# RMS statistics by column groups of TensorE, spread over the partitions by two fp32r products per half

## The chip, the cores and the metric

The kernel runs on one NeuronCore of a Trainium2 chip. The metric is the time of one execution on the device in microseconds. Three timed runs of the kernel before gave 932.94, 933.66 and 934.06 us; the median is 933.66 us.

## The reference

One layer of a two-branch trunk over 1024 tokens of width 1024. What matters here are its two RMS norms, one ahead of everything else and one near the end:

```python
def rms_norm(x, g):
    xf = x.astype(jnp.float32)
    y = xf * lax.rsqrt(jnp.mean(xf * xf, axis=-1, keepdims=True) + NORM_EPS)
    return (y * g.astype(jnp.float32)).astype(x.dtype)

h = rms_norm(x, g_pre[i])
proj = h @ w_in[i]
...
x = x + rms_norm(merged @ w_out[i], g_post[i])
x = x + (p[i] @ w_ple[i]) * jax.nn.sigmoid(x @ w_ple_gate[i])
```

Between them stand the S5 and RG-LRU branches, their projections and gates, which the change leaves alone.

## The kernel before

Activations lie transposed: features over the 128 partitions, tokens along the free dimension, so a row tile of 128 features is 128x1024, and most work goes by halves of 512 tokens. Every large product is made of three fp32r products of 512 columns (`three`, L314 to L318): each operand is split into a rounded high part and a low remainder, and high x high, high x low and low x high are summed in PSUM. Weights come as quads of four 128x128 blocks. ScalarE makes a quad's high part (L222); its remainder comes from VectorE (L234, `lows`) or, for some late weights, from a second copy on ScalarE (L225) followed by an accumulating DMA that GpSimd issues (L226). A quad is prepared four quads ahead of its use.

TensorE, VectorE, ScalarE and GpSimd execute in the order in which the program is written; nothing reorders them. Work that is to run beside products is written as generators, of which `tick()` advances each by one step after a group of products. Only the order of SyncE's DMA issues is chosen by a scheduler.

The mean over features of a norm is a sum over partitions. `tok_rstd` (L383) does it in three steps, separated by `yield`:

1. `pst`: for each 128 tokens one product with the squares `ssq` as the stationary operand and one column of ones as the moving one (L388). The sums of 128 tokens then lie down the 128 partitions of one PSUM column: 128x8 for 1024 tokens, 128x4 for 512.
2. The reciprocal root of these few columns on VectorE and ScalarE: scale and EPS (L392), square root (L393, ScalarE), reciprocal (L394), a Newton step (L395 to L398). Then for each 128 tokens a diagonal matrix of the result (L401).
3. `psb`: ones times each diagonal (L406), which puts the value of each token into all 128 partitions of a PSUM bank, 512 tokens a bank.

It is called in three places.

**Before the first norm** (name `pre`, both halves at once). The squares of the 8 row tiles of `x` are summed on VectorE by seven additions (L710). Meanwhile TensorE computes the eight rows of `p @ w_ple` (`ps_ple`, m = 0 to 7, 12 products each) as filler. Step 1 stands behind row 5, step 3 in the middle of row 7. The rows rotate through three PSUM buffers `pw2`, so row 7 needs the buffer of row 4, which ScalarE must have copied out (`evict(4)`, L740), and the first `ps_u` needs that of row 5. The schedule of ScalarE and VectorE in this stretch is a table:

```python
            4: ((Q, 3), (E, 3)),
            5: ((E, 4), (Q, 4)),
            6: ((E, 5), (Q, 5), (Q, 6)),
```

`Q` prepares a weight quad (L222 and L234), `E` is `evict`. After step 3, `h_hi` scales `x` (L724, VectorE) and makes its high part (L725, ScalarE), `h_lo` its remainder (L730), and the `ps_u` products follow.

**Before the second norm**, by halves of tokens (`post1`, then `post0`), in the generator `post_half`: step 1 and 2 in one tick, step 3 one tick later, which is 12 products of TensorE. Half 1 runs beside the last products `oV` of the output projection; from step 3 on, VectorE normalises, adds the residual and splits eight row tiles (L1559, L1560, L1368, `x1hl`), for which the first gate products `ps_pg` wait. Half 0 runs beside the gate products of half 1, whose sigmoids (L1586) and their use (L1587, L1588) share the engines with it. The square root and the sigmoid need different tables on ScalarE, each loaded by an instruction of its own.

The diagonals of the second norm lie in one page, `diags`.

## Time and profile before

| What | Value |
| --- | --- |
| Median of three runs | 933.66 us (932.94 to 934.06) |
| The profiled execution's own time | 932.99 us |
| Its span, from first to last instruction | 931.2 us |
| VectorE busy | 624.4 us (67%) |
| ScalarE busy | 470.3 us (51%) |
| GpSimd busy | 150.5 us (16%) |
| DMA, mean over the span | 144 GB/s |

The time is 1.8 us longer than the span: that is what lies around the first and the last instruction. A row of the timeline gives the start in the span, the busy time, the engine, the line of the kernel, the instruction, what it writes and reads, the shape and the count of merged instructions, and in brackets for how long the engine stood idle before it and what ended that. An fp32 product shows as two passes in the trace, an fp32r product as one. TensorE's instructions overlap, so their durations are longer than the step from one start to the next.

### The profile page before, as it was taken

Reading aid. Unit: us, or ns where it says so; the run is one execution under the profiler, and the core shown is the slowest. Engines: PE = TensorE matmul, PEld = TensorE weight load, DVE = VectorE, ACT = ScalarE, POOL = GpSimd, SP = SyncE. Lnnn points to the kernel's source line nnn. Section 1 sums busy time; section 2 is a strip of 40 time slices with the busy share of each in tenths; the row PEclk is TensorE's granted clock in tenths of the full one; section 3 lists DMA queues with packets and bytes.
Section 4 is the critical chain, followed back from the end, with each engine's and each line's share of the span. In section 5 each row is a group of like instructions: output and inputs, shape, how many; then the busy total and the mean of one; then the engine's idle time right before and its main releaser. Section 6 shows DMA issues by size and latency. Waiting matters only on the chain.

```text
span 931.2 us, 11720 instructions
## 1 busy us (share of the span) xinstructions
PE 923.2 (99%) x4232; PEld 759.2 (82%) x4232; DVE 624.4 (67%) x974; ACT 470.3 (51%) x714; POOL 150.5 (16%) x159
## 2 busy tenths in 40 slices
PE   8999999999999999999999999999999999999998
PEld 7888888888888888888888888888888887887876
DVE  6885566666664446776666667687862798886863
ACT  6643233444443356666666668544524355558531
POOL 1217112212220000000000000022322126422100
PEclk9999999999999999999999999999999999999999
DMA  9745445554523201111111116811479975499951
GB/s 342 288 126 159 123 144 165 175 166 135 175 95 109 74 29 52 51 50 47 52 51 51 52 39 210 299 39 57 140 259 243 251 180 204 121 244 230 305 176 55
DMA packets 70442, 134.21 MB, mean 144 GB/s; under 512 B 18416, under 2 KB 32880, under 8 KB 70384
## 3 DMA queue, kind: packets, MB, share of 16 engines
q1 hardware_dynamic: 64912, 122.98, 41.3%
q0 software_dynamic: 5472, 10.49, 6.4%
q8 instruction: 33, 0.54, 0.2%
q14 instruction: 25, 0.20, 0.1%
HBM read 95.30 MB, written 27.53 MB: 132 GB/s over the span
## 4 chain that ended last, share of the span: by engine, by line
PE 95%; DVE 3%; DMA 1%; issue 1%; SPq 0%; ACT 0%; DVEq 0%
PE ps_L L318 16%; PE ps_L L316 8%; PE ps_rx L318 8%; PE ps_rg L318 8%; PE ps_pg L318 6%; PE ps_rg L316 4%; PE ps_rx L316 4%; PE ps_F L318 3%; PE ps_u L318 3%; PE bZ L318 3%; PE ps_pg L316 3%; PE pg L318 2%; PE bW L318 2%; PE bX L318 2%; PE ps_ea L318 2%; PE ps_eb L318 2%
## 5 line engine op out<-in xcount | busy, mean ns | idle before, releaser
L318 PE MATMUL ps_L<-hB,wq 128*128 128x512 f32 x640 | 197.4, 390 | 0.0
L318 PEld LDWEIGHTS ps_L<-hB,wq 128*128 128x128 f32 x640 | 120.2, 188 | 24.5
L316 PE MATMUL ps_L<-hB,wq 128*128 128x512 f32 x320 | 127.0, 397 | 0.0
L222 ACT ACTIVATE wq<-wraw 128x512 fp32r<-128x512 f32 (+1 forms) x188 | 112.5, 614 | 23.5 <-issue 9.4
L234 DVE TENSOR_TENSOR wq<-wraw,wq 128x512 fp32r<-128x512 f32 (+1 forms) x152 | 104.2, 701 | 6.4 <-ACT wq L222 6.4
L318 PE MATMUL ps_rx<-hB,wq 128*128 128x512 f32 x320 | 98.6, 390 | 0.0
L318 PE MATMUL ps_rg<-hB,wq 128*128 128x512 f32 x320 | 98.6, 390 | 0.0
L318 PE MATMUL ps_pg<-x1hl,wq 128*128 128x512 f32 x240 | 75.2, 394 | 0.5 <-DVE x1hl L1368 0.5
L316 PEld LDWEIGHTS ps_L<-hB,wq 128*128 128x128 f32 x320 | 60.1, 188 | 13.4 <-issue 1.7
L318 PEld LDWEIGHTS ps_rg<-hB,wq 128*128 128x128 f32 x320 | 60.1, 188 | 12.9
L318 PEld LDWEIGHTS ps_rx<-hB,wq 128*128 128x128 f32 x320 | 60.1, 188 | 12.9
L1072 DVE SCALAR_TENSOR_TENSOR c<-ps_rx,cp_t,c 128x1023 f32<-128x1023 f32 (+2 forms) x30 | 38.5, 1282 | 47.6 <-ACT c L1070 46.9
L194 POOL TENSOR_TENSOR wS<-wraw 128x512 f32<-128x512 f32 x8 | 12.1, 1510 | 356.4 <-DMA wraw<-w_blocks 344.9
L316 PE MATMUL ps_rx<-hB,wq 128*128 128x512 f32 x160 | 62.5, 391 | 0.0
L316 PE MATMUL ps_rg<-hB,wq 128*128 128x512 f32 x160 | 62.5, 391 | 0.0
L318 PEld LDWEIGHTS ps_pg<-x1hl,wq 128*128 128x128 f32 x240 | 44.7, 188 | 11.9 <-DVE x1hl L1368 1.9
L1009 ACT ACTIVATE sg<-ps_L 128x1024 f32<-128x1024 f32 x20 | 20.5, 1027 | 59.6 <-issue 52.4
L226 POOL DMA_DIRECT2D wq<-wraw x36 | 31.8, 882 | 100.7 <-ACT wq L225 68.7
L316 PE MATMUL ps_pg<-x1hl,wq 128*128 128x512 f32 x120 | 47.1, 393 | 0.0
L318 PE MATMUL ps_u<-hB,wq 128*128 128x512 f32 x128 | 39.8, 392 | 0.4 <-DVE hB L730 0.4
L318 PE MATMUL ps_F<-ys,wq 128*128 128x512 f32 x128 | 39.4, 389 | 0.0
L1080 ACT ACT_TABLE_LOAD x9 | 11.5, 1283 | 51.2 <-DVE yr L1109 51.2
(355 smaller groups left out, 1929.7 us busy)
## 6 DMA issues: line engine op xcount, KB each, us to landing
wraw<-w_blocks SPq DMA_DIRECT2D x95, 512.0 KB
wq<-wraw POOLq DMA_DIRECT2D x36, 256.0 KB, 5.8
xt<-x_t SPq DMA_DIRECT2D x8, 512.0 KB
ple_d<-ple_sb SPq DMA_DIRECT2D x8, 512.0 KB
wn<-sbt SPq DMA_DIRECT2D x8, 512.0 KB
sgl_d<-sg SPq DMA_DIRECT2D x8, 512.0 KB
wn<-pt_d SPq DMA_DIRECT2D x16, 256.0 KB
sgs_d<-sg SPq DMA_DIRECT2D x8, 512.0 KB
```

The lines of the kernel that those rows point to most:

```text
L194: G.tensor_tensor(s[name], s[a], s[b], op)
L222: nc.scalar.activation(hi, src, AF.Copy)
L226: nc.gpsimd.dma_start(lo.bitcast(F32), src, accum_op=ALU.add)
L234: self.nc.vector.tensor_tensor(lo, src, hi.bitcast(F32), ALU.subtract)
L316: T.matmul(ps, wh, xh, start=start, stop=False, skip_group_check=more)
L318: T.matmul(ps, a, b, start=False, stop=stop and a is (wh if xl_last else wl), skip_group_check=more)
L1009: S.activation(t, ps, AF.Sigmoid)
L1072: V.scalar_tensor_tensor(c[:, d:], ps[:, :NT - d], w_[3 - d], c[:, d:], ALU.mult, ALU.add)
L1080: S.activation(sq, ps, AF.Sigmoid)
```

## The change

The layout of the statistics is turned round. The sums no longer lie down the partitions but along the free dimension, with ones as the stationary operand and the squares as the moving one:

```diff
-        for c in range(nch):
-            for j, ssq in enumerate(ssqs):
-                T.matmul(ps[:, c:c + 1], ssq[:, c * P:(c + 1) * P], ones[:, 0:1], start=j == 0, stop=j == len(ssqs) - 1)
+        for h in range(nh):
+            for j, src in enumerate(srcs):
+                for c in range(4):
+                    T.matmul(ps[32 * c:32 * c + 32, h * P:(h + 1) * P], ones[:, :32],
+                             src[:, h * HT + c * P:h * HT + (c + 1) * P],
+                             start=j == 0, stop=j == len(srcs) - 1, tile_position=(0, 32 * c), skip_group_check=True)
```

Each product fills 32 partitions of PSUM from one of four groups of 32 columns of the array: tokens 0 to 127 of a half go to partitions 0 to 31, the next 128 to partitions 32 to 63, and so on, every sum 32 times over. The result is 128x128 for a half, 128x256 for both. In the first norm the squares of rows 6 and 7 are no longer added on VectorE but enter as further products: `srcs` has three members, so there are 24 products in place of 8. In the second norm it is four in place of four.

The reciprocal root is then taken of the whole 128x128 or 128x256, in PSUM, by the same instructions:

```diff
-        V.tensor_scalar(var, ps[:, :nch], 1.0 / (ND * P), EPS, ALU.mult, ALU.add)
-        S.activation(sd, var, AF.Sqrt)
-        V.reciprocal(r, sd)
-        V.tensor_tensor(t, r, r, ALU.mult)
-        V.tensor_tensor(t, t, var, ALU.mult)
+        n = nh * P
+        var, t, r = ps[:, :n], ps[:, n:2 * n], r[:, :n]
+        V.tensor_scalar(var, var, 1.0 / (ND * P), EPS, ALU.mult, ALU.add)
+        S.activation(t, var, AF.Sqrt)
+        V.reciprocal(r, t)
+        V.tensor_tensor(t, var, r, ALU.mult)
+        V.tensor_tensor(t, t, r, ALU.mult)
         V.tensor_scalar(t, t, -0.5, 1.5, ALU.mult, ALU.add)
         V.tensor_tensor(r, r, t, ALU.mult)
```

In place of the diagonals, the result is split into an fp32r high part (ScalarE) and a remainder (VectorE) in pieces of 32 partitions x 128, each put at the columns of its tokens in a block of zeros; two fp32r products of 512 columns with a matrix of 1/32 (`sel`) then sum over the partitions and so give every partition the value of each token:

```diff
-        for c in range(nch):
-            V.tensor_scalar(diag[:, c, :], ident, r[:, c:c + 1], None, ALU.mult)
-        yield
-        for h in range(n // HT):
+        for h in range(nh):
+            for c in range(4):
+                s_, cs = slice(32 * c, 32 * c + 32), slice(h * HT + c * P, h * HT + (c + 1) * P)
+                rc = r[s_, h * P:(h + 1) * P]
+                S.activation(hi[s_, cs], rc, AF.Copy)
+                V.tensor_tensor(lo[s_, cs], rc, hi[s_, cs].bitcast(F32), ALU.subtract)
+        yield
+        for h in range(nh):
             pb = px.tile([P, HT], F32, tag="px", name=f"psb_{name}_{h}")
-            for c in range(4):
-                T.matmul(pb[:, c * P:(c + 1) * P], ones, diag[:, 4 * h + c, :], start=True, stop=True)
+            T.matmul(pb, sel, hi[:, h * HT:(h + 1) * HT], start=True, stop=False)
+            T.matmul(pb, sel, lo[:, h * HT:(h + 1) * HT], start=False, stop=True)
```

GpSimd makes `sel` and zeroes the blocks: 128x2048 at the start of the program (page 7, so that the parameters `braw` of the same page are allocated and loaded after the first norm), 128x1024 ahead of the second norm.

ScalarE at the first norm, from the eviction of row 3 (`ps_ple3`) on; `wq` are weight quads. Before:

```order
L740 ACTIVATE ple_sb5_116<-ps_ple3_246 128x1024
L393 ACTIVATE rs_pre_180<-rs_pre_180 128x8
L740 ACTIVATE ple_sb13_117<-ps_ple4_266 128x1024
L222 ACTIVATE wq4_323<-wraw4_196 128x512
L740 ACTIVATE ple_sb13_117<-ps_ple5_284 128x1024
L222 ACTIVATE wq5_341<-wraw4_196 128x512
L222 ACTIVATE wq6_344<-wraw5_220 128x512
```

And after the change, the same place on ScalarE:

```order
L753 ACTIVATE ple_sb5_118<-ps_ple3_250 128x1024
L398 ACTIVATE pst_pre_299<-pst_pre_299 128x256
L409 ACTIVATE spread_122<-sdp_111 32x128 x8
L753 ACTIVATE ple_sb13_119<-ps_ple4_268 128x1024
L222 ACTIVATE wq4_349<-wraw4_200 128x512
L753 ACTIVATE ple_sb13_119<-ps_ple5_286 128x1024
L222 ACTIVATE wq5_367<-wraw4_200 128x512
L222 ACTIVATE wq6_370<-wraw5_224 128x512
```

The eight copies of the high part stand ahead of the eviction of row 4, which before followed the square root at once; they read the end of VectorE's arithmetic.

VectorE at the same place, from the remainder of quad 3 to the first scaling of `x` (L724, now L737). Before:

```order
L234 TENSOR_TENSOR wq3_279<-wraw3_165,wq3_279 128x512
L392 TENSOR_SCALAR rs_pre_180<-pst_pre_297 128x8
L394 RECIPROCAL rs_pre_180<-rs_pre_180 128x8
L395 TENSOR_TENSOR rs_pre_180<-rs_pre_180 128x8
L396 TENSOR_TENSOR rs_pre_180<-rs_pre_180 128x8
L397 TENSOR_SCALAR rs_pre_180<-rs_pre_180 128x8
L398 TENSOR_TENSOR rs_pre_180<-rs_pre_180 128x8
L401 TENSOR_SCALAR sdp_109<-ident_88,rs_pre_180 128x128 x8
L234 TENSOR_TENSOR wq4_323<-wraw4_196,wq4_323 128x512
L234 TENSOR_TENSOR wq5_341<-wraw4_196,wq5_341 128x512
L234 TENSOR_TENSOR wq6_344<-wraw5_220,wq6_344 128x512
L724 SCALAR_TENSOR_TENSOR xt0_107<-xt0_107,cp_t_95,psb_pre_0_354 128x512
```

After:

```order
L397 TENSOR_SCALAR pst_pre_299<-pst_pre_299 128x256
L399 RECIPROCAL sdp_111<-pst_pre_299 128x256
L400 TENSOR_TENSOR pst_pre_299<-pst_pre_299,sdp_111 128x256
L401 TENSOR_TENSOR pst_pre_299<-pst_pre_299,sdp_111 128x256
L402 TENSOR_SCALAR pst_pre_299<-pst_pre_299 128x256
L403 TENSOR_TENSOR sdp_111<-sdp_111,pst_pre_299 128x256
L410 TENSOR_TENSOR spread_122<-sdp_111,spread_122 32x128 x8
L234 TENSOR_TENSOR wq4_349<-wraw4_200,wq4_349 128x512
L234 TENSOR_TENSOR wq5_367<-wraw4_200,wq5_367 128x512
L234 TENSOR_TENSOR wq6_370<-wraw5_224,wq6_370 128x512
L737 SCALAR_TENSOR_TENSOR xt0_109<-xt0_109,cp_t_97,psb_pre_0_380 128x512
```

The count is the same and the place too; each step is 128x256 in place of 128x8, and the eight subtractions each follow one of ScalarE's copies. The remainders of quads 4 to 6 still stand between them and the first scaling.

ScalarE at half 0 of the second norm, where `sbp` is the sigmoid of a gate product. Before:

```order
L393 ACT_TABLE_LOAD
L393 ACTIVATE diags<-diags 128x4
L1586 ACT_TABLE_LOAD
L1586 ACTIVATE sbp<-ps_pg_1_6690 128x512
L222 ACTIVATE wq_6748<-wraw_6581 128x512
```

After:

```order
L398 ACT_TABLE_LOAD
L398 ACTIVATE pst_post_6753<-pst_post_6753 128x128
L409 ACTIVATE spreads<-r_post 32x128 x4
L1600 ACT_TABLE_LOAD
L1600 ACTIVATE sbp<-ps_pg_1_6717 128x512
```

The table load for the sigmoid and the sigmoid itself, which before followed the square root, now follow the four copies.

More of the change, by code (lines that the diff above doesn't have):

```diff
@@ L295, in tile_hybrid_trunk @@
     ident = cst([P, P], "ident")
+    sel = cst([P, P], "sel", dt=F32R)
+    r_post = cst([P, P], "r_post")
     make_identity(nc, ident)
@@ L381, in rows, with tok_rstd @@
         return ps
-    def tok_rstd(v, ssqs, n, name, res, diag):
-        nch = n // P
+    def tok_rstd(r, srcs, n, name, res, spread):
+        nh = n // HT
         ps = px.tile([P, HT], F32, tag="px", name=f"pst_{name}")
-        for c in range(nch):
-            for j, ssq in enumerate(ssqs):
-                T.matmul(ps[:, c:c + 1], ssq[:, c * P:(c + 1) * P], ones[:, 0:1], start=j == 0, stop=j == len(ssqs) - 1)
-        yield
-        v = v.rearrange("p (i n) -> p i n", i=4)
-        var, r, t, sd = (v[:, i, :nch] for i in range(4))
-        V.tensor_scalar(var, ps[:, :nch], 1.0 / (ND * P), EPS, ALU.mult, ALU.add)
-        S.activation(sd, var, AF.Sqrt)
-        V.reciprocal(r, sd)
-        V.tensor_tensor(t, r, r, ALU.mult)
-        V.tensor_tensor(t, t, var, ALU.mult)
+        for h in range(nh):
[4 more added lines that the diff above has]
+                             start=j == 0, stop=j == len(srcs) - 1, tile_position=(0, 32 * c), skip_group_check=True)
+        yield
+        n = nh * P
[5 more added lines that the diff above has]
+        V.tensor_tensor(t, t, r, ALU.mult)
@@ L397, in tok_rstd @@
         V.tensor_scalar(t, t, -0.5, 1.5, ALU.mult, ALU.add)
         V.tensor_tensor(r, r, t, ALU.mult)
-        diag = diag.rearrange("p (c t) -> p c t", c=nch)
-        for c in range(nch):
-            V.tensor_scalar(diag[:, c, :], ident, r[:, c:c + 1], None, ALU.mult)
+        hi, lo = spread
+        for h in range(nh):
[4 more added lines that the diff above has]
+                V.tensor_tensor(lo[s_, cs], rc, hi[s_, cs].bitcast(F32), ALU.subtract)
@@ L476, in tile_hybrid_trunk @@
     pt = scratch[:, :NPT]
-    braw = page(7, "braw", F32)
+    spread = page(7, "spread").rearrange("p (i n) -> p i n", i=2)
     ET = mybir.EngineType
@@ L490, in tile_hybrid_trunk @@
     tq = sk.tile([P, 4, 32], F32, name="tq")
+    G.tensor_scalar(sel, ones, 1.0 / 32.0, None, ALU.mult)
+    zeros = spread.rearrange("p i n -> p (i n)")
+    G.memset(zeros.bitcast(F32), 0.0)
+    G.tensor_copy(zeros, zeros.bitcast(F32))
     G.memset(toep, 0.0)
@@ L705, in square @@
         if k:
-            adds.append(sq)
+            (adds if k < 6 else srcs).append(sq)
     def add_squares(left):
@@ L712, in tile_hybrid_trunk @@
     rb = []
-    ssqs = [ssq]
-    stats = tok_rstd(pro.tile([P, 4 * ND], F32, name="rs_pre"), ssqs, NT, "pre", rb, sdp[:, 1])
+    srcs = [ssq]
+    stats = tok_rstd(sdp[:, 1], srcs, NT, "pre", rb, (spread[:, 0], spread[:, 1]))
     hq = {}
@@ L778, in tile_hybrid_trunk @@
     h_hi(1)
+    braw = page(7, "braw", F32)
     nc.sync.dma_start(braw[:, :1024], spar[:, NPT:NPT + 1024])
@@ L1546, in post_half @@
         add_square(h)
-        st = tok_rstd(dg[:, 2, 32 * h:32 * h + 32], [ssq[h]], HT, f"post{h}", out_, dg[:, h, :])
+        st = tok_rstd(r_post, [ssq[h]], HT, f"post{h}", out_, (dg[:, 0, :], dg[:, 1, :]))
         if h == 0:
@@ L1601, in gate_half @@
                 finish(ps, cs)
-    dg = quarter(page(PG[1], "diags", F32))
+    dg = quarter(page(PG[1], "spreads"))
+    G.memset(dg[:, :2, :].bitcast(F32), 0.0)
+    G.tensor_copy(dg[:, :2, :], dg[:, :2, :].bitcast(F32))
     bg.append(post_half(1))
```

## The prediction

> **What bounds the kernel now.** The page's head comes first.

> ```profile
> span 931.2 us, 11720 instructions
> PE 923.2 (99%) x4232; PEld 759.2 (82%) x4232; DVE 624.4 (67%) x974; ACT 470.3 (51%) x714; POOL 150.5 (16%) x159
> ```

> TensorE (PE) is busy for 923.2 of 931.2 us. So what lengthens or shortens TensorE's own row of work counts in full, a new wait of TensorE counts in full, and there are no later waits in which a delay could vanish. What the other engines do counts only where TensorE comes to wait for it. I therefore read the timeline at the three places of the change, and ask at each what TensorE meets next. The first norm:

> ```profile
> 22.43 2.55 DVE L710 TENSOR_TENSOR sdp<-sdp,sqs 128x1024 f32<-128x1024 f32 x2
> 25.04 1.95 PE L388 MATMUL pst_pre<-ones,sdp 128*128 128x1 f32 x16
> 26.84 0.48 PE L316 MATMUL ps_ple<-p_hi,wq 128*128 128x512 f32 x1
> 27.02 0.17 DVE L392 TENSOR_SCALAR rs_pre<-pst_pre 128x8 f32<-128x8 f32 x1 [1.43 <-PE pst_pre L388]
> 27.22 0.21 ACT L393 ACTIVATE rs_pre<-rs_pre 128x8 f32<-128x8 f32 x1 [3.49 <-DVE rs_pre L392]
> 27.34 1.01 ACT L740 ACTIVATE ple_sb<-ps_ple 128x1024 f32<-128x1024 f32 x1
> 28.51 1.67 DVE L401 TENSOR_SCALAR sdp<-ident,rs_pre 128x128 f32<-128x128 f32 x8
> 29.67 1.15 ACT L222 ACTIVATE wq<-wraw 128x512 fp32r<-128x512 f32 x2
> 30.08 1.90 DVE L234 TENSOR_TENSOR wq<-wraw,wq 128x512 fp32r<-128x512 f32 x3
> 31.04 1.95 PE L406 MATMUL psb_pre<-sdp,ones 128*128 128x128 f32 x16
> 32.13 1.64 DVE L724 SCALAR_TENSOR_TENSOR xt<-xt,cp_t,psb_pre 128x512 f32<-128x512 f32 x2 [0.15 <-PE psb_pre L406]
> 39.29 0.74 PE L318 MATMUL ps_u<-hB,wq 128*128 128x512 f32 x2 [0.40 <-DVE hB L730]
> ```

> The whole arithmetic (27.02 to 30.18) lies beside 18 row products, 26.84 to 31.04, 0.233 us each, and TensorE never waits for it. Two things depend on it closely. The eviction of row 4 (27.34) frees the buffer that row 7 takes 12 products after 26.84, at 29.64. And the chain from L724 (32.13) over ScalarE and L730 to the second pair of `ps_u` products already ends in a wait of TensorE at 39.29: when L724 moves, TensorE moves by as much.

> **The change: the first norm.** Dropping two additions gains nothing, since TensorE gets to `pst` at 25.04 in its own order and the last addition had just ended (24.98). For products on column groups there is a row, the S5 branch's four fp32 products with 16 columns each; beside it a copy of their result, and the widths that the arithmetic will have:

> ```profile
> 120.03 0.41 PE L922 MATMUL pkt<-ca,bb 128*16 128x128 f32 x8
> 120.56 1.11 ACT L925 ACTIVATE kt<-pkt 16x128 f32<-16x128 f32 x4 [6.47 <-issue]
> L1587 DVE TENSOR_TENSOR sbp<-sbp,plp 128x256 f32<-128x256 f32 x2 | 0.9, 426 | 3.2 <-ACT sbp L1586 3.2
> L1586 ACT ACTIVATE sbp<-ps_pgz 128x256 f32<-128x256 f32 x2 | 0.8, 384 | 4.7 <-PE ps_pgz L318 4.7
> L394 DVE RECIPROCAL diags<-diags 128x4 f32<-128x4 f32 x2 | 0.4, 178 | 0.6 <-ACT diags L393 0.6
> L557 DVE RECIPROCAL scratch<-scratch 128x10 f32<-128x10 f32 x1 | 0.2, 216 | 0.0
> L638 DVE RECIPROCAL scratch<-scratch 128x32 f32<-128x32 f32 x1 | 0.4, 356 | 8.7 <-POOL scratch L636 8.7
> ```

> - Sums. Eight passes take 0.41 us where 16 full ones take 1.95 (L406, 0.12 a pass), so the groups do overlap. The 24 products are six such rounds, but a group must do its rounds one after the other: 0.41 + 5 x 2 passes x 0.12 = 1.61 us. Below: one pass a round, 1.01; above: six rounds with no overlap, 2.46. I take 1.61. Row 6 starts at 26.65 (before 26.84), VectorE 0.18 later as before, at 26.83.
> - Arithmetic. 0.03 us lie between dependent steps (27.19 to 27.22). Variance, 128x256: 0.46 with its gap. Square root 0.38 + 0.03. **The reciprocal** is the odd one: 178, 216 and 356 ns for 4, 10 and 32 elements is 6.3 to 6.4 ns an element, where the other operations need about 1. For 256 that is 0.178 + 252 x 0.00636 = 1.78 us. The Newton step: 4 x 0.46. Sum 0.46 + 0.41 + 1.81 + 1.84 = 4.52, so the result is there at 31.35. [...]
> - Copies. Eight 32x128 copies on ScalarE: 0.28 us each by L925, 0.20 by the 128-wide L401. I take 0.24: 1.92 us (1.6 to 2.2). They end at 33.27; the last subtraction 0.3 later, no longer on the path.
> - What is behind them. The eviction of row 4 starts at 33.27 in place of 27.34 and ends at 34.28. TensorE reaches row 7 at 26.65 + 2.80 = 29.45 and **waits 4.8 us**. ScalarE then does what it did before: from that eviction to the high part of quad 6 took 29.67 + 1.15 - 27.34 = 3.48, so 36.75. L234 for quad 6 stands ahead of L724: + 0.65, L724 at 37.4. The spreading products, four of 0.233 in place of 16 passes, are done near 36.3 and bind no more. L724 shifts by 37.4 - 32.13 = **5.3 us**, and TensorE with it. With the bounds of products and copies 4.4 to 6.4.

> [...]

> **The second norm.**

> ```profile
> 819.34 1.28 ACT L393 ACT_TABLE_LOAD   x1
> 819.44 0.95 PE L388 MATMUL pst_post<-ones,ssq 128*128 128x1 f32 x8
> 823.11 1.05 PE L406 MATMUL psb_post<-diags,ones 128*128 128x128 f32 x8
> 824.20 0.69 DVE L1559 TENSOR_TENSOR mix<-mix,psb_post 128x512 f32<-128x512 f32 x1 [0.85 <-PE psb_post L406]
> 842.63 0.73 PE L318 MATMUL ps_pg<-x1hl,wq 128*128 128x512 f32 x2 [0.48 <-DVE x1hl L1368]
> ...
> 857.91 0.95 PE L388 MATMUL pst_post<-ones,ssq 128*128 128x1 f32 x8
> 859.31 1.28 ACT L1586 ACT_TABLE_LOAD   x1
> 860.61 0.60 ACT L1586 ACTIVATE sbp<-ps_pg 128x512 f32<-128x512 f32 x1
> 861.24 0.69 DVE L1587 TENSOR_TENSOR sbp<-sbp,plp 128x512 f32<-128x512 f32 x1
> 861.54 1.05 PE L406 MATMUL psb_post<-diags,ones 128*128 128x128 f32 x8
> 862.53 0.86 POOL L226 DMA_DIRECT2D wq<-wraw  x1 [3.90 <-PE psb_post L406]
> 862.63 0.69 DVE L1559 TENSOR_TENSOR mix<-mix,psb_post 128x512 f32<-128x512 f32 x1
> 866.85 0.70 DVE L1587 TENSOR_TENSOR sbp<-sbp,plp 128x512 f32<-128x512 f32 x1 [0.76 <-ACT sbp L1586]
> 872.83 0.69 DVE L1587 TENSOR_TENSOR sbp<-sbp,plp 128x512 f32<-128x512 f32 x1 [0.58 <-ACT sbp L1586]
> 879.41 0.69 DVE L1587 TENSOR_TENSOR sbp<-sbp,plp 128x512 f32<-128x512 f32 x1 [0.58 <-ACT sbp L1586]
> 886.06 0.73 PE L318 MATMUL ps_pg<-x1hl,wq 128*128 128x512 f32 x2
> ```

> *Half 1.* Sums 0.41, so VectorE starts at 820.03; the square root still waits for its table, to 820.64. It takes 0.28 (L925) + 0.03; the reciprocal 0.178 + 124 x 0.00636 = 0.97 + 0.03; four steps of 0.29 + 0.03 (L401's 128 wide, 0.29): 823.23. The fourth copy starts 0.72 later; with copy, gap and subtraction the products can start at 824.58 in place of 823.11, 1.47 later. They are 0.5 shorter (two of 0.233 for eight passes of 0.12), so what follows on TensorE and L1559 on VectorE shift by **1.0 us** (0.6 to 1.4). From L1559 VectorE works almost without a gap up to the wait at 842.63, so nothing is made up.

> *Half 0.* The result is there at 861.41, the last copy ends at 862.4, and the sigmoid, whose table load is now behind the copies, starts at 863.7 in place of 860.61. L1559 stands on VectorE behind two steps that need this sigmoid, so it slips from 862.63 to 865.7, 3.1 us. On the way to 886.06 VectorE stood idle for 0.76 + 0.58 + 0.58 = 1.9 us, which it uses up; 1.2 are left. TensorE itself slips by 0.7 at the spreading products (1.2 late, 0.5 shorter). The later one counts: **1.2 us** (0.7 to 1.8).

> GpSimd's zeroing of 128x2048 is costed at nothing: it falls between 1.9 and 14.0 us, when that engine has no work (its next row, L702 at 14.00, waited 12.07 us for a DMA), and before the second norm the weight DMAs behind it are four quads, some 11 us, ahead of use. Were VectorE slowed meanwhile, up to 0.5 us. SyncE's order changes only among loads and stores with no reader near.

> **Sum.** 5.3 + 1.0 + 1.2 = 7.5 on the profiled execution's 932.99: 940.5. The median of the runs is 0.67 above that execution, so 941.2 us; its own range, from the bounds, 939.5 to 943.

> **Rivals.**

> *TensorE comes back slow after the 4.8 us wait.* At the start of the program it ran at half pace:

> ```profile
> 1.05 4.64 PE L497 MATMUL warm<-ones 128*128 128x128 f32 x20 [1.05 <-DVE halfpi L291]
> ```

> That is 0.23 a pass against 0.12 later. If this came back for some 4 us, row 7's half (6 products) and the first spreading pair would end at 34.28 + 8 x 0.47 = 38.0, L724 at 38.3 in place of 37.4, and `ps_u` up to 0.5 later still: 0.9 to 1.4 more, 942.4. The granted clock in the page says full speed throughout, even at the start, so it cannot decide. The trace of before has no wait as long as this. [...] Chance 0.20.

> *Late weight remainders.* ScalarE's second copies at half 0 slip with the sigmoid, so L226 goes from 862.53 to some 865.6, and its DMA is needed four quads on, at the third product: 863.2 + 3 x 2.80 + 0.47 = 872.1. These 36 DMAs land after 5.8 us at the median, the slowest here after 8.8: in time at the median, up to 2.3 late at worst, of which half is hidden by the 1.2 already counted. 942.5, chance 0.10.

> *The reciprocal is flat* and costs 0.43 for 256: 1.35 less in the first norm, 0.7 in each half: 938.5. Against it stand three widths on one line. Chance 0.07.

> *The column groups do not overlap with 32 columns*: 48 passes of 0.12 are 5.8 in place of 1.6, and 0.5 more in each half: 946.5. L922 speaks against it. Chance 0.05.

> *No slower.* If an operation's width cost nothing and each of the fifteen steps to the eviction took about 0.21 as the narrow ones, the result came at 28.3, the eviction started at 30.0, L724 at 34.1: + 2.0. In the second norm both chains would hide again and the shorter products be gained: - 0.5 and - 0.3. 934.9, within 0.2% (1.9 us, what a measurement here can tell from no change). It decides once the mean step falls below 0.26 us. The 426 and 384 ns rows speak against it. Chance 0.03.

> **How the numbers follow.** The forecast has 0.55. The range takes in the slow return and the late remainders (0.85 with it): their upper ends, on the products' upper bound, carry it to 944.0, and the low end, 938.3, is where the flat reciprocal would come out. Slower by over 0.2%: all but the last case, 0.96; within 0.2%: 0.03; faster: 0.01.

> **What would show it.** Right: a wait of TensorE of 4 to 5 us ahead of row 7, ended by the eviction; a RECIPROCAL row of 128x256 near 1.8 us and two of 128x128 near 1.0; L737 near 37.4; `pst_pre` over about 1.6 us; sigmoid and L1573 some 3 us late at half 0. Wrong: row 7 starting without a wait, products at half pace behind it, or a wait on a weight quad after 870.

## The result, and the profile after

Four timed runs of the changed kernel gave 944.46, 944.98, 945.24 and 945.68 us, a median of 945.11 us; four of the kernel before gave 932.94, 932.99, 933.66 and 934.06, a median of 933.33 us. The ratio is 1.0126 with a 95% interval of 1.0114 to 1.0138: **slower by 11.8 us**. The forecast had the sign, but with 941.2 us only two thirds of the loss, and the time lies above its range.

The head of the page after, with the share and the instructions of each engine:

```profile
span 943.2 us, 11754 instructions
PE 923.6 (98%) x4240; PEld 755.5 (80%) x4240; DVE 630.3 (67%) x972; ACT 476.2 (50%) x730; POOL 156.3 (17%) x164
```

The span grew by 12.0 us, TensorE's busy time by 0.4. So the loss is not work of TensorE but idle time, and it can be read from TensorE's waits. The timeline of the changed kernel in the first norm (start and duration in us, engine, line, operation; in brackets the idle time before it and what ended it):

```profile
26.28 0.43 DVE L397 TENSOR_SCALAR pst_pre<-pst_pre 128x256 f32<-128x256 f32 x1 [3.18 <-PE pst_pre L391]
27.15 1.76 DVE L399 RECIPROCAL sdp<-pst_pre 128x256 f32<-128x256 f32 x1 [0.43 <-ACT pst_pre L398]
...
30.34 0.42 DVE L403 TENSOR_TENSOR sdp<-sdp,pst_pre 128x256 f32<-128x256 f32 x1
30.79 2.63 ACT L409 ACTIVATE spread<-sdp 32x128 fp32r<-32x128 f32 x8 [3.68 <-DVE sdp L403]
...
33.45 1.02 ACT L753 ACTIVATE ple_sb<-ps_ple 128x1024 f32<-128x1024 f32 x1
...
34.52 0.80 PE L318 MATMUL ps_ple<-p_hi,wq 128*128 128x512 f32 x1 [5.32 <-ACT ple_sb L753]
...
36.59 1.29 DVE L234 TENSOR_TENSOR wq<-wraw,wq 128x512 fp32r<-128x512 f32 x2 [0.74 <-ACT wq L222]
...
38.34 1.48 DVE L737 SCALAR_TENSOR_TENSOR xt<-xt,cp_t,psb_pre 128x512 f32<-128x512 f32 x2 [0.46 <-PE psb_pre L415]
```

The reader sees the forecast's chain in its order: sums, arithmetic with a reciprocal of 1.76 us, eight copies on ScalarE, the eviction of row 4, a wait of TensorE of 5.32 us ahead of row 7, and L737 at 38.34 where L724 stood at 32.13. One thing is new in this stretch, and the windows of the trace show it (busy time and instructions of each engine, then the granted clock, DMA share and GB/s):

```profile
28.50:31.90 3.40, 0.70 (x4) 0.23 (x2) 2.78 (x8) 1.03 (x4) 0.00 (x0) 1.00 0.35 135
31.90:38.80 6.90, 4.28 (x10) 3.41 (x11) 4.04 (x10) 5.03 (x10) 0.00 (x0) 0.51 0.45 160
38.80:42.20 3.40, 3.40 (x15) 2.45 (x15) 3.37 (x6) 2.98 (x4) 0.00 (x0) 1.00 0.78 246
```

From 31.9 to 38.8 us the granted clock is 0.51. Row 7's products of 512 columns start every 0.43 us in it, in place of 0.23. The two halves of the second norm, in the same timeline:

```profile
825.85 0.43 PE L391 MATMUL pst_post<-ssq,ones 128*32 128x128 f32 x8
...
829.62 1.30 ACT L409 ACTIVATE spreads<-r_post 32x128 fp32r<-32x128 f32 x4 [2.41 <-DVE r_post L403]
...
831.07 0.47 PE L414 MATMUL psb_post<-spreads,sel 128*128 128x512 f32 x1 [1.84 <-ACT spreads L409]
...
850.30 0.73 PE L320 MATMUL ps_pg<-x1hl,wq 128*128 128x512 f32 x2 [0.51 <-DVE x1hl L1382]
...
864.10 0.50 PE L320 MATMUL ps_pg<-x1hl,wq 128*128 128x512 f32 x1 [0.64 <-DMA wq<-wraw]
...
866.61 0.43 PE L391 MATMUL pst_post<-ssq,ones 128*32 128x128 f32 x8
...
871.40 0.51 PE L414 MATMUL psb_post<-spreads,sel 128*128 128x512 f32 x1 [1.38 <-ACT spreads L409]
...
872.66 0.60 ACT L1600 ACTIVATE sbp<-ps_pg 128x512 f32<-128x512 f32 x1
...
874.63 0.68 DVE L1573 TENSOR_TENSOR mix<-mix,psb_post 128x512 f32<-128x512 f32 x1
...
877.72 0.62 ACT L1375 ACTIVATE x1hl<-x 128x512 fp32r<-128x512 f32 x1
878.24 0.58 ACT L1600 ACTIVATE sbp<-ps_pg 128x512 f32<-128x512 f32 x1
...
878.85 0.69 DVE L1601 TENSOR_TENSOR sbp<-sbp,plp 128x512 f32<-128x512 f32 x1 [0.76 <-ACT sbp L1600]
...
882.88 0.75 DVE L1574 SCALAR_TENSOR_TENSOR x<-mix,cp_t,x 128x512 f32<-128x512 f32 x1
...
883.67 0.63 ACT L1375 ACTIVATE x1hl<-x 128x512 fp32r<-128x512 f32 x1 [0.31 <-DVE x L1574]
884.21 0.58 ACT L1600 ACTIVATE sbp<-ps_pg 128x512 f32<-128x512 f32 x1
...
884.82 0.69 DVE L1601 TENSOR_TENSOR sbp<-sbp,plp 128x512 f32<-128x512 f32 x1 [0.58 <-ACT sbp L1600]
...
898.05 0.73 PE L320 MATMUL ps_pg<-x1hl,wq 128*128 128x512 f32 x2 [1.63 <-DVE x1hl L1382]
```

Half 1 goes as forecast: the spreading products wait 1.84 us, and the later wait for `x1hl` at 850.30 is the old one of 842.63, moved. At half 0 the wait at 898.05 has no counterpart of its size before (886.06, with no wait shown), and VectorE's idle 0.76 us, which was to be used up, still stands at 878.85.

To compare runs, four stages are cut at TensorE's own instructions: the first `pst_pre` product, the last `ps_u` product, the first `pst` product of half 1, that of half 0, and the last product of all. What happens ahead of the first (it came between 24.7 and 25.8 us in these runs, and 0.34 earlier after than before) is left out.

| Run, us | first norm | middle | half 1 | half 0 |
| --- | --- | --- | --- | --- |
| before | 53.42 | 740.99 | 38.47 | 68.54 |
| after | 59.80 | 741.35 | 40.77 | 71.81 |
| E1 first norm only | 59.92 | 740.96 | 39.06 | 68.53 |
| E2 second norm only | 53.43 | 741.93 | 40.63 | 71.81 |
| E3 row 4 evicted ahead | 59.12 | 741.55 | 41.31 | 71.80 |
| E4 before, VectorE delayed | 53.31 | 740.97 | 38.45 | 69.78 |
| E5 TensorE kept busy | 59.12 | 741.07 | 40.67 | 71.81 |
| E6 no copies | 53.84 | 741.07 | 38.94 | 68.53 |
| E7 no correction steps | 58.03 | 741.07 | 39.16 | 70.39 |
| E8 no copies, row 4 ahead | 53.81 | 741.07 | 38.92 | 68.79 |
| E9 copies last | 56.52 | 741.08 | 40.40 | 71.82 |
| E10 no copies, three steps | 53.35 | 741.08 | 38.52 | 68.70 |

After less before: 6.38 + 0.36 + 2.30 + 3.27, less the 0.34 of the earlier start, is 11.97 us, the growth of the span. The forecast had 5.3, 0, 1.0 and 1.2. So the last term was the furthest off.

### The profile page after: what moved, and what is told of

Its sections match the earlier page's. It is cut to its first block, busy times and chain, and to the rows that moved or that the text cites. A ratio compares the mean times of both kernels' runs of the same rounds, so it can differ in the third digit from the quotient of the medians.

```text
span 943.2 us, 11754 instructions
## 1 busy us (share of the span) xinstructions
PE 923.6 (98%) x4240; PEld 755.5 (80%) x4240; DVE 630.3 (67%) x972; ACT 476.2 (50%) x730; POOL 156.3 (17%) x164
## 4 chain that ended last, share of the span: by engine, by line
PE 84%; DVE 7%; issue 3%; DMA 3%; ACT 2%; POOL 1%; SPq 0%; ACTq 0%; DVEq 0%; POOLq 0%
PE ps_L L320 15%; PE ps_L L318 8%; PE ps_rg L320 8%; PE ps_rx L320 8%; PE ps_pg L320 4%; PE ps_rg L318 4%; PE ps_rx L318 4%; PE ps_u L320 3%; PE bZ L320 3%; PE ps_pg L318 2%; PE pg L320 2%; PE bW L320 2%; PE bX L320 2%; PE ps_ea L320 2%; PE ps_eb L320 2%
## 5 line engine op out<-in xcount | busy, mean ns | idle before, releaser
L318 PE MATMUL ps_L<-hB,wq 128*128 128x512 f32 x320 | 127.0, 397 | 0.0
L222 ACT ACTIVATE wq<-wraw 128x512 fp32r<-128x512 f32 (+1 forms) x188 | 112.7, 614 | 23.6 <-issue 9.4
L234 DVE TENSOR_TENSOR wq<-wraw,wq 128x512 fp32r<-128x512 f32 (+1 forms) x152 | 105.5, 710 | 9.0 <-ACT wq L222 9.0
L318 PEld LDWEIGHTS ps_L<-hB,wq 128*128 128x128 f32 x320 | 60.1, 188 | 13.4 <-issue 1.7
L318 PE MATMUL ps_rg<-hB,wq 128*128 128x512 f32 x160 | 62.5, 391 | 0.0
L318 PE MATMUL ps_rx<-hB,wq 128*128 128x512 f32 x160 | 62.5, 391 | 0.0
L226 POOL DMA_DIRECT2D wq<-wraw x36 | 31.9, 886 | 104.5 <-ACT wq L225 87.4
L318 PE MATMUL ps_pg<-x1hl,wq 128*128 128x512 f32 x120 | 47.1, 393 | 0.0
```

What stands on the lines that cost most here:

```text
L222: nc.scalar.activation(hi, src, AF.Copy)
L226: nc.gpsimd.dma_start(lo.bitcast(F32), src, accum_op=ALU.add)
L234: self.nc.vector.tensor_tensor(lo, src, hi.bitcast(F32), ALU.subtract)
L318: T.matmul(ps, wh, xh, start=start, stop=False, skip_group_check=more)
```

## The experiments

After the trace of the changed kernel the working theory (A in most of the expectations) was that every delay counts in full, at half 0 too, where the prediction had taken VectorE's idle time for slack.

**E1 and E2: each norm alone.** `tok_diag` is the old `tok_rstd` under another name.

```diff
-        st = tok_rstd(r_post, [ssq[h]], HT, f"post{h}", out_, (dg[:, 0, :], dg[:, 1, :]))
+        st = tok_diag(dg[:, 2, 32 * h:32 * h + 32], [ssq[h]], HT, f"post{h}", out_, dg[:, h, :])
```

That is E1. E2:

```diff
-            (adds if k < 6 else srcs).append(sq)
+            adds.append(sq)
-    stats = tok_rstd(sdp[:, 1], srcs, NT, "pre", rb, (spread[:, 0], spread[:, 1]))
+    stats = tok_diag(pro.tile([P, 4 * ND], F32, name="rs_pre"), ssqs, NT, "pre", rb, sdp[:, 1])
```

> New form in the first norm only, old form in both halves of the second. Theory A (what the trace of after shows): the products of the second weight pair of ps_u start at 45.3 us, 6.0 us later than before, and everything behind them moves rigidly: 933.3 + 6.1 = 939.4 us, and no wait of TensorE on a weight remainder after 850 us, because nothing near the second norm has changed its relative order. Theory B (the place of the DMAs in time, set by the first norm's shift, makes the remainder late): the 0.64 us wait appears here too, 940.4 us. The prediction's own term for this part was 5.3, so 938.6 us.

> Old form in the first norm, new form in both halves of the second. Theory A (VectorE's idle time at half 0 is the delay of a loop over ScalarE, not slack, so its 3.3 us slip counts in full): 1.3 + 3.3 = 4.6 with no wait on a weight remainder, 937.9 us; with that wait another 1.0, 938.9 us. Rival, the prediction's account (1.9 us of the slip absorbed): 1.0 + 1.2 = 2.2, 935.5 us, up to 936.5 with the wait.

E1: 940.29 us (939.27 to 941.03) against 933.19; ratio 1.0074 (1.0059 to 1.0089). E2: 939.38 us (937.84 to 939.49); ratio 1.0059 (1.0042 to 1.0076). The stages add up: the first norm's loss is E1's alone (59.92), that of half 0 is E2's alone (71.81 to the hundredth). The prediction's 935.5 for the second norm is out. E2's median lies above theory A's 937.9 and 938.9 as well; in its profile 0.94 us more than before are in the middle stage, where VectorE waits for a DMA, and some 0.7 us of its half 1 are a drop of the clock (both below). In E1, where nothing near the second norm has changed, TensorE nevertheless waits for a weight remainder at the place of 864.10:

```profile
862.98 0.50 PE L319 MATMUL ps_pg<-x1hl,wq 128*128 128x512 f32 x1 [0.31 <-DMA wq<-wraw]
```

So a wait on a DMA at this place can come with nothing more than the shift in time that the first norm makes, as theory B had it (940.4 us), though here of half the size.

**E4: is VectorE's idle time at half 0 slack?** The kernel before, and two additions on a scratch quarter of a page.

```diff
+        if h == 0:
+            for _ in range(2):
+                V.tensor_tensor(dg[:, 3, :], dg[:, h, :], dg[:, h, :], ALU.add)
         for k in range(ND):
             mk = mixt(k, h)
             V.tensor_tensor(mk, mk, rb, ALU.mult)
```

> The kernel before, with two additional VectorE additions of 128x512 (0.69 us each, 1.4 us together, on a scratch page) in front of the first multiplication by the norm of half 0, and nothing else. Theory A (loop): the 0.76, 0.58 and 0.58 us idle times of VectorE stay, and the end moves by 1.3 to 1.4 us: 934.7 us. Rival (slack of 1.9 us, as the prediction took it): the delay is absorbed, the idle times shrink to about 0.5 in all, and the time stays at 933.3 us.

934.59 us (934.09 to 934.93) against 933.19; ratio 1.0013 (1.0004 to 1.0023). The half-0 stage grew by 1.24 us for 1.33 us put in (862.92 to 864.25). VectorE's rows in the timeline of E4, at the three places where it was idle before (866.85, 872.83 and 879.41), and TensorE's wait that ends the chain:

```profile
868.46 0.69 DVE L1590 TENSOR_TENSOR sbp<-sbp,plp 128x512 f32<-128x512 f32 x1 [0.76 <-ACT sbp L1589]
...
874.43 0.69 DVE L1590 TENSOR_TENSOR sbp<-sbp,plp 128x512 f32<-128x512 f32 x1 [0.58 <-ACT sbp L1589]
...
881.01 0.69 DVE L1590 TENSOR_TENSOR sbp<-sbp,plp 128x512 f32<-128x512 f32 x1 [0.58 <-ACT sbp L1589]
...
887.66 0.73 PE L318 MATMUL ps_pg<-x1hl,wq 128*128 128x512 f32 x2 [1.26 <-DVE x1hl L1368]
```

The idle times are what they were, 0.76, 0.58 and 0.58. They are the length of a loop, which the changed kernel's rows from 882.88 on show: VectorE's L1601 (884.82) waits for a sigmoid, the sigmoid (884.21) stands in ScalarE's queue behind a high part of `x1hl` (883.67), and that waited for VectorE's L1574 (882.88). The wait of 0.76 us at 878.85 is of the same kind, with two weight quads more in ScalarE's queue. Whatever moves VectorE moves the sigmoid with it.

**E3: the eviction of row 4 taken ahead.**

```diff
         if m == 5:
             next(stats)
+            evict(4)
             next(stats)
-            5: ((E, 4), (Q, 4)),
+            5: ((Q, 4),),
```

> The changed kernel with one thing moved: row 4 is evicted after the sums have been issued and ahead of the square root. Theory A: TensorE no longer waits 5.3 us ahead of row 7, only about 2 us for the spread rows; its clock stays whole there; and ScalarE's work behind the copies comes 1.0 us earlier, so that VectorE's last weight remainder ends at 36.8 and the first L737 starts near 36.9 in place of 38.34: 1.5 us less than after, 943.6 us. Rival (the first norm's loss is TensorE's wait itself, 5.3 us): most of it comes back, 940 to 941 us.

944.46 us (942.80 to 945.84); ratio 1.0118 (1.0103 to 1.0134). The first norm got 0.68 shorter, less than either expected. The wait of 5.32 us went, and others came:

```profile
33.04 0.47 PE L414 MATMUL psb_pre<-spread,sel 128*128 128x512 f32 x1 [1.68 <-ACT spread L409]
...
39.07 0.49 PE L318 MATMUL ps_u<-hB,wq 128*128 128x512 f32 x1 [2.59 <-ACT hB L738]
```

L737 came at 37.56, 12.06 after the start of the sums in place of 13.65. TensorE had less left to do by then, and its granted clock fell here too, to 0.50 from 40.4 to 43.7, so that of 1.6 us gained at L737 only 0.68 arrived. TensorE's wait for row 4 was a symptom: what is late is the work behind the copies.

**E5: the wait filled with products.**

```diff
+        if m == 7 - 1:
+            fill = px.tile([P, HT], F32, tag="px", name="fill")
+            for _ in range(20):
+                T.matmul(fill[:, :P], ones, ones, start=True, stop=True)
```

> The changed kernel with 20 additional fp32 products of 128x128 by 128x128 (0.24 us each, 4.9 us together), whose result nobody reads, between the products of row 6 and of row 7, where TensorE waited 5.3 us. Theory A (the half pace after the wait costs only what stands between the end of VectorE's last weight remainder, 37.88, and the first spreading pair, 38.34): row 7 and the spreading products run at full pace, L737 starts at 37.9, and 0.5 us is gained: 944.6 us. Rival (the half pace costs what the prediction's rival gave it, 0.9 to 1.4 us): 943.7 to 944.2 us. If the pace is still halved, the wait is not its cause.

944.87 us (944.11 to 946.86); ratio 1.0126 (1.0111 to 1.0142). In E5 the granted clock stays whole there (1.00 from 31.9 to 38.8). In its timeline the spreading products now end by 37.3, and L737 follows VectorE's remainder:

```profile
34.71 0.50 PE L318 MATMUL ps_ple<-p_hi,wq 128*128 128x512 f32 x1 [0.85 <-ACT ple_sb L753]
...
36.78 1.29 DVE L234 TENSOR_TENSOR wq<-wraw,wq 128x512 fp32r<-128x512 f32 x2 [0.74 <-ACT wq L222]
...
37.99 1.40 DVE L737 SCALAR_TENSOR_TENSOR xt<-xt,cp_t,psb_pre 128x512 f32<-128x512 f32 x2
```

The first norm's stage is 0.68 us shorter than after. So the half pace was real, came from the wait, and cost 0.7 us: near theory A's 0.5, and less than the rival's 0.9 to 1.4. The median of the runs cannot show this: the half-1 stage is 0.70 us longer than it would be but for a second drop of the clock (the last section).

**E6 and E8: no copies.** The wide result is spread by fp32 products against four constant matrices; E8 takes row 4's eviction ahead as well, as in E3.

```diff
-        hi, lo = spread
-        for h in range(nh):
-            for c in range(4):
...
-                S.activation(hi[s_, cs], rc, AF.Copy)
-                V.tensor_tensor(lo[s_, cs], rc, hi[s_, cs].bitcast(F32), ALU.subtract)
...
-            T.matmul(pb, sel, hi[:, h * HT:(h + 1) * HT], start=True, stop=False)
-            T.matmul(pb, sel, lo[:, h * HT:(h + 1) * HT], start=False, stop=True)
+            for c in range(4):
+                T.matmul(pb[:, c * P:(c + 1) * P], sel[:, c], r[:, h * P:(h + 1) * P], start=True, stop=True)
```

> The changed kernel without the hi and lo copies: the wide result is spread by four fp32 products per half against four constant matrices that hold 1/32 in the rows of one group. 8 pairs of small copies go in the first norm and 4 in each half; the spreading products take 1.95 and 0.97 us in place of 0.93 and 0.47. Theory A (all of the chain's length counts, behind it nothing has slack): row 4's eviction starts at 30.8 in place of 33.45, L737 at 35.7 in place of 38.34, so 2.65 us less; half 1 1.0 less (1.5 earlier, 0.5 longer); half 0 3.1 less, because the sigmoid's table load then follows the square root directly: 938.4 us. Rival (the copies are beside the path, and the reciprocal and the wide steps carry the loss): within 1.5 us of the changed kernel, 943.5 to 945.5 us.

> The kernel without copies with row 4 evicted ahead of the square root as well. Theory A (in the first norm the path goes over ScalarE's queue: copies and eviction ahead of the weight quads, then VectorE's three remainders, then L737): VectorE's remainders follow the arithmetic directly, L737 starts near 32.8, TensorE waits less than 1 us ahead of the spreading products: 2.9 us less than without the copies alone, 935.5 us. Rival (the row-4 eviction brings as little here as it did beside the copies, 0.65 us): 937.8 us.

E6: 934.92 us (934.33 to 936.03) against 933.38; ratio 1.0017 (1.0008 to 1.0027). E8: 934.69 us (934.08 to 935.19); ratio 1.0013 (1.0003 to 1.0022). Without the copies 10.2 of the 11.8 us are gone. At half 0 the 3.1 us expected came (71.81 to 68.53), and half 1 gave 1.83, of which 0.8 is a late weight remainder that is not there in E6. In the first norm 5.96 us came back in place of 2.65, so theory A's sum was wrong by 3.3 us. The timeline of E6 shows why:

```profile
27.89 0.37 ACT L401 ACTIVATE pst_pre<-pst_pre 128x256 f32<-128x256 f32 x1 [3.49 <-DVE pst_pre L400]
28.17 1.02 ACT L746 ACTIVATE ple_sb<-ps_ple 128x1024 f32<-128x1024 f32 x1
...
30.50 1.16 ACT L222 ACTIVATE wq<-wraw 128x512 fp32r<-128x512 f32 x2
...
33.62 1.40 DVE L730 SCALAR_TENSOR_TENSOR xt<-xt,cp_t,psb_pre 128x512 f32<-128x512 f32 x2
```

I had let the eviction follow VectorE's result, as the copies did. Without copies nothing on ScalarE waits for that result any more: eviction and weight quads follow the square root at 28.17, beside the reciprocal. And as the eviction is early by itself, E8's move of it has nothing left to gain (53.84 and 53.81), against my 2.9 us and the rival's 0.65.

**E7: the correction steps left out.**

```diff
-        V.tensor_tensor(t, var, r, ALU.mult)
-        V.tensor_tensor(t, t, r, ALU.mult)
-        V.tensor_scalar(t, t, -0.5, 1.5, ALU.mult, ALU.add)
-        V.tensor_tensor(r, r, t, ALU.mult)
```

> The changed kernel without the four VectorE steps of the correction of the reciprocal square root (so the result is the less exact value of the square root and the reciprocal). Theory A: each step counts in full wherever it stands, 4 x 0.46 = 1.85 us in the first norm and 4 x 0.33 = 1.33 in each half: 945.1 - 4.5 = 940.6 us. Rival (1.9 us of VectorE's time at half 0 is slack, so half 0 gains at most what TensorE waits at its spreading products, 1.38): no more than 3.2 to 4.0 us gained in all, and the gain at half 0 shows at the spreading products but not at the later wait for x1hl.

940.63 us (939.95 to 942.70) against 933.38; ratio 1.0081 (1.0065 to 1.0098): 4.5 us less than after, as theory A had it. By stages: 1.77 in the first norm, 1.61 in half 1 (with a wait for a weight remainder that is 0.3 shorter), 1.42 in half 0, where the steps took 1.33 us. The rival allowed half 0 only a gain at the spreading products; the gain is at the end of the chain.

**E9: the copies behind the evictions and quads.** A `yield` ahead of the copies, taken after the work of row 6 in the first norm and at once in the second.

```diff
+        yield
         hi, lo = spread
...
+        if m == 6:
+            next(stats)
```

> The changed kernel with the eight pairs of small copies of the first norm put behind the evictions of rows 4 and 5 and the weight quads 4 to 6 in the order of ScalarE and VectorE; nothing is left out and the second norm is as in the changed kernel. Theory A (most of what the copies cost in the first norm, 5.9 us by the run without them, is that evictions and quads stand in ScalarE's queue behind copies that wait 3.7 us for VectorE's result, and not the copies' own 2.6 us): the evictions and quads run from 27 to 30.5 us beside the reciprocal, TensorE waits for the spread rows alone, the subtractions of the copies end near 35.2 behind VectorE's three remainders, and L737 starts near 35.2 in place of 38.34: 3.1 us less than the changed kernel, 942.0 us. Rival (the copies' own length on the path is the cost, wherever they stand): within 0.7 us of the changed kernel, 944.4 to 945.1 us.

942.23 us (941.61 to 942.94) against 933.51; ratio 1.0093 (1.0077 to 1.0108). That is theory A's 942.0. 3.28 us of the first norm's 6.38 went by this order alone, with every copy still there. The clock has a share in it: it was at half for 3.41 us here (34.67 to 38.08, at 0.50) and for 6.83 in the changed kernel, and E5 prices the whole of that at 0.7 us. ScalarE and VectorE in the timeline of E9:

```profile
27.77 1.02 ACT L754 ACTIVATE ple_sb<-ps_ple 128x1024 f32<-128x1024 f32 x1
...
30.11 1.16 ACT L222 ACTIVATE wq<-wraw 128x512 fp32r<-128x512 f32 x2
31.54 2.63 ACT L410 ACTIVATE spread<-sdp 32x128 fp32r<-32x128 f32 x8 [0.28 <-DVE sdp L403]
...
33.23 2.48 DVE L411 TENSOR_TENSOR spread<-sdp,spread 32x128 fp32r<-32x128 f32 x8
35.74 1.60 DVE L738 SCALAR_TENSOR_TENSOR xt<-xt,cp_t,psb_pre 128x512 f32<-128x512 f32 x2
```

Evictions and quads fill the 3.7 us in which ScalarE stood waiting at 30.79 in the changed kernel. What is left of the copies' price is their own length, now on VectorE ahead of L738: E9's stage is 2.68 us longer than E6's, which has no copies.

**E10: three steps in place of four**, on E8. It computes everything.

```diff
-        V.tensor_tensor(t, var, r, ALU.mult)
+        V.scalar_tensor_tensor(t, var, -0.5, r, ALU.mult, ALU.mult)
         V.tensor_tensor(t, t, r, ALU.mult)
-        V.tensor_scalar(t, t, -0.5, 1.5, ALU.mult, ALU.add)
-        V.tensor_tensor(r, r, t, ALU.mult)
+        V.scalar_tensor_tensor(r, t, 1.5, r, ALU.add, ALU.mult)
```

> The kernel without copies and with row 4 ahead, with the correction of the reciprocal square root written in three VectorE steps in place of four (two of them take a scalar and a second tensor in one instruction). Theory A (every step of the chain counts in full also here): 0.46 us less in the first norm and 0.33 in each half, 1.1 us in all, 933.6 us, and so as fast as the kernel before within what can be measured. Rival (without the copies the chain is again beside TensorE's work, as in the kernel before): no gain, 934.7 us.

934.09 us (933.36 to 935.38, eleven runs) against 933.51 us (fifteen runs); ratio 1.0005 (0.9996 to 1.0013), the same within the measurement. The first norm's stage is 0.46 shorter than E8's and half 1 by 0.40, as expected; half 0 only by 0.09 in place of 0.33, where a wait of 0.58 us for a weight remainder stands at 871.68. This is the fastest form of the change that I found; none was faster than the kernel before.

## Why the prediction was wrong, point by point

- **Sums: right.** `pst_pre` took 1.44 us (24.70 to 26.14; forecast 1.61), so the column groups do overlap. The rival of no overlap is out, and so is the flat reciprocal of 0.43 (the 426 ns of a product of that width): 1.76 and 0.96 us against 1.78 and 0.97. The arithmetic took 4.48 us, from 26.28 to 30.76, against 4.52.
- **Copies: the mechanism right, the size outside its bounds.** Eight took 2.63 us and four 1.30, 0.33 each; I took 0.24 between 0.20 and 0.28. The 0.20 came from L401, which is an instruction of VectorE and no price for ScalarE; the 0.28 came from ScalarE's L925, copies of 16 partitions of fp32 out of PSUM to fp32. That is 0.7 us in the first norm. It is not VectorE's subtractions between the copies that slow them: in E9 the eight took 2.63 us as well, and VectorE began the first subtraction (33.23) only when five of them were done. What else it is was not tried.
- **The clock: the rival came as well.** It had 0.20 for a drop after the 4.8 us wait. The granted clock was 0.51 from 31.9 to 38.8, and the price was 0.7 us (E5) in place of 0.9 to 1.4. With the copies' 0.7 this takes 5.3 to 6.7; 6.38 was measured, or 6.56 at L737. That half pace would last some 4 us was an assumption that no run shows: it lasted 6.83 us here and 3.4 in E3 and E9. The drop came behind a stretch of 3.40 us in which TensorE was busy for 0.70.
- **Half 1: right.** 1.26 us at the wait for `x1hl` (24.45 from `pst_post` to it in place of 23.19) against 1.0, the four longer copies being the rest.
- **Half 0: the step that failed** is "On the way to 886.06 VectorE stood idle for 0.76 + 0.58 + 0.58 = 1.9 us, which it uses up". The slip itself was sized well: from `pst_post` to L1573 it is 8.02 us in place of 4.72, 3.3 against the 3.1 forecast. But nothing of it was used up. E4 shows that these idle times do not take up a delay, E2, E3, E5 and E9 give the same 71.8 with the copies as they are, and E6 and E7 give the time back when the chain gets shorter. The term was 3.27 in place of 1.2. This alone puts the forecast at 943.3, which is still inside its range: the copies' 0.7, the clock's 0.7 and the late remainder's 0.8 (next point) are what carry the time beyond 944.0.
- **Late weight remainders: in part.** The waits on weight quads after 870 came (0.34 at 881.21; 2.0 in E5, none in E3) and cost nothing, as the half-0 stage is 71.8 with and without them: the chain to 898.05 was later still. The one that costs is earlier, at 864.10: the product starts 1.03 us after the one ahead of it in place of 0.23, so 0.8 us. The DMA that it waited for was issued at 856.34 and landed after 7.71 us; its counterpart before, issued at 848.66, landed after 5.84. In E1 a shift in time brought a late one at this place too; why that DMA takes longer then is open. (The rival's own sum was 0.2 too high: 2.3 late less the 1.2 counted is 1.1, so 942.3 in place of 942.5.)
- **What no term had:** 0.36 us in the middle. There VectorE waits for a DMA of `msr` (L1431); in three of the twelve profiles this stage is longer than 741.08, by up to 0.9, in the other nine it is 740.96 to 741.08. Seven of the ten profiles with the new form in one norm or both do not have it, so it is a transfer that lands late at times; whether the change makes it likelier is not shown.

The terms measured: 6.38 + 0.36 + (1.26 + 0.80 + 0.24 of smaller shifts) + 3.27 - 0.34 = 11.97.

What the list above does not say is why the first norm lost so much in the first place. The prediction took the place of the copies in ScalarE's queue as given and added up the lengths. E9 shows that about half of the loss, 3.28 of 6.38 us (of it up to 0.7 by the clock), is that place: an instruction that waits 3.7 us for VectorE, with ready work behind it. Of the rest 2.68 is the copies' own length (E9 against E6). The wide arithmetic, which was the longest item in the prediction's sum, costs no more than 0.42 us where nothing on ScalarE waits for its end (E6 against before).

## What to carry to other kernels

Idle time of an engine is slack only if what it waits for would come no later when the engine itself is late; follow the releaser back, and if the way leads through the same engine, it is a loop and every delay counts in full. When a change puts a new instruction on an engine that takes its instructions in program order (row 4's eviction on ScalarE ran at 33.45 behind the copies and at 27.77 ahead of them, in E9), ask first how long it will wait and what ready work stands behind it; its duration is only a part of its price (here 2.7 us of 6.0). And a layout that makes statistics cheaper for TensorE (here 1.44 us from the first sum to the next product, in place of 1.80) can make them wide for VectorE (here 4.5 us of arithmetic from the variance to the result, in place of 1.5).

## What the runs showed of the hardware

```profile
822.95:826.36 3.41, 1.57 (x8) 0.97 (x7) 2.69 (x9) 1.99 (x6) 0.00 (x0) 1.00 1.05 266
...
826.40:829.70 3.30, 3.30 (x10) 2.52 (x9) 3.23 (x6) 2.02 (x4) 0.86 (x1) 0.50 0.78 196
```

The window of the changed kernel that holds most of its wait, that of E9, with the same wait and no drop, and one of E5 with a wait of 2.02 us for a weight remainder and no drop:

```profile
827.25:830.66 3.41, 1.98 (x9) 1.30 (x7) 2.73 (x8) 0.96 (x4) 0.00 (x0) 1.00 0.99 286
...
826.56:829.97 3.41, 1.71 (x7) 1.42 (x8) 2.76 (x8) 2.38 (x6) 0.39 (x1) 1.00 0.92 214
...
878.34:881.75 3.41, 1.65 (x8) 1.03 (x6) 3.34 (x6) 1.58 (x4) 0.86 (x1) 1.00 1.09 255
```

With TensorE busy for 1.57 of 3.41 us the clock fell (also at half 1 in E3, 1.58, and E5, 1.57), with 1.65, 1.71 and 1.98 it did not. So it went with how a wait lay on the grid: behind one and the same wait of 1.83 or 1.84 us the clock fell in three profiles of five. The busy share alone does not tell the cases apart, though. At the start of the program the clock also fell in E4 and E6, behind windows with 1.72 and 2.00 us busy (at 8.05 and 7.83; in E6 to 0.50, and the mean granted clock of both profiled executions is 0.998); why is open. In E2, E3 and E5 the drop made the half-1 stage some 0.7 us longer (40.63 in E2, which has no late remainder there, against 40.77 less 0.80 for the changed kernel). As the grid lies differently from run to run, this may be one reason why four runs of such a kernel scatter over 1.2 to 3.0 us, where 13 to 19 runs of the kernel before scatter over 0.9 to 1.6; that is not shown.

GpSimd's clearing of the spread page at the start was costed at nothing, but something was beside it: VectorE's first weight remainder (4.20) took 2.07 us while GpSimd ran (L502 and L503, 1.96 to 5.72), against 0.69 before. It is 2.00 to 2.12 in the six profiles with the clearing and 0.69 in the six without. TensorE waited 0.85 us for it at 6.33. The first `pst_pre` product still came 0.34 us earlier than before, and over the twelve profiles that time varies by 1.1 us without regard to the clearing, so no cost of it can be told.
